# Splitting the store of the last group but one into unequal shares for the DMA engines

## The chip, the cores and the metric

The kernel runs on one core of one Trainium2 chip. The metric is the device time of one execution in microseconds: 209.35 us before the change, the median of 3 runs (209.31 to 209.42). The core has five engines that run their own instruction streams: PE (matrix multiplication), DVE, ACT and POOL (element-wise work) and SP, which here only issues transfers. Behind SP's queue stand 16 DMA engines that move the data between the chip's main memory (DRAM) and the on-chip memory of 128 partitions.

## The reference

```python
x        = randn(16, 512, 1024)   # float32
weight   = randn(1024, 768)
bias     = randn(768)
residual = randn(16, 512, 768)
out = (np.matmul(x, weight) + bias + residual).astype(np.float32)
```

Flattened, it is a product of 8192 x 1024 by 1024 x 768, to which a row (the bias) and a matrix of 8192 x 768 (the residual) are added.

## The kernel before

The 8192 rows are cut into 64 tiles of 128 rows (`n_sub`), eight of which make a group (`G = 8`, eight groups). Row p x 8 + j of a group lies in partition p, so that tile j of the group has one row in each partition, and the eight rows of a partition are contiguous in DRAM. One transfer of a group's residual or output therefore moves 128 pieces, one for each partition, of 8 x 768 x 4 = 24,576 bytes.

For each half group (four tiles) ACT casts x to bfloat16 (`cast_x`, L121), DVE transposes blocks of 32 x 32 (`transpose_blocks`, `transpose_and_move`, L152 to L161), ACT moves half of the blocks into place (`move_blocks`, L126), and PE multiplies with the weights (L307 to L326), tile by tile, into one of four PSUM buffers. DVE adds the PSUM buffers to the residual in place, two tiles at a time (`evacuate`, L163), and POOL adds the bias to the same place (`add_bias`, L212), two tiles at a time, 32 times in all. Tiles 62 and 63 get their bias before PE is done with them (addition 29, L224), so that the last step is DVE's. The place that held the residual then holds the output and is stored from there.

Every transfer is issued by SP, in the order of a list written by hand (`ORDER`, L17). A name such as `x5`, `r7` or `st6` stands for the load of x, the load of the residual or the store of that group; a letter stands for a part of its tiles, by `PARTS` and, for group 7, by `LAST_PARTS`: `st7a` is tiles 0 to 3, `st7b` 4 and 5, `st7c` 6 and 7. `st4+` stores groups 4 and 5 in one transfer. The loop at L240 takes the names in turn, lets SP wait for what the transfer needs, and issues it at L286. A store waits until POOL has counted its additions up to the last tile of the part (L278: the semaphore `add`, against the number kept in `added` for that tile), and the very last store waits for DVE (L276). All stores from group 3 on raise one semaphore, `st`, by 16 each (L284); the kernel ends when it has reached its full count (`late`, L35 and L39). Between the loads and the stores nothing else orders the transfers: SP's instructions run in order, and the DMA engines work through what they were given.

Of the kernel before, what the change touches and what calls it, by code (L numbers as in the profile page):

```python
# [11 lines left out]
P = 128  # L12
# [2 lines left out]
B = 4  # L15

ORDER = ("x0a w0 bias w1 x0b r0 x1a x1b r1 x2 r2 x3 r3 x4 st0 "  # L17
         "st1 r4 x5 r5 st2 x6a x6b r6 x7 r7 st3 st4+ st6 st7a st7b st7c").split()
PARTS = {"": (0, 8), "a": (0, 4), "b": (4, 8)}
LAST_PARTS = {"a": (0, 4), "b": (4, 6), "c": (6, 8)}  # L20


@with_exitstack
def kernel(
    ctx: ExitStack,
    tc: tile.TileContext,
    x: bass.AP,
    weight: bass.AP,
    bias: bass.AP,
    residual: bass.AP,  # L30
    out: bass.AP,
):
    nc = tc.nc
    stored = ctx.enter_context(nc.semaphore("st"))
    late = 16 * sum(name[:2] == "st" and int(name[2]) > 2 for name in ORDER)  # L35
    nc.scalar.sem_inc(stored, late)
    with tc.tile_critical(name="all", no_gpsimd_drain=True):  # L37
        emit(nc, ctx, x, weight, bias, residual, out, stored, late)
    nc.sync.wait_ge(stored, late)  # L39


def emit(nc, es, x, weight, bias, residual, out, stored, late):
# [8 lines left out]
    n_grp = n_sub // G  # L51
    n_bat = n_sub // B
    chunks = [(0, 512), (512, N - 512)]
    sp, act, dve, pool, pe = nc.sync, nc.scalar, nc.vector, nc.gpsimd, nc.tensor
# [18 lines left out]
    def sem(name):  # L73
        if name not in sems:
            sems[name] = es.enter_context(nc.semaphore(name))
        return sems[name]

    def wait(eng, name, value):
        eng.wait_ge(sem(name), value)  # L79
# [14 lines left out]
    def group(ap, g):  # L94
        return ap[g * G * P:(g + 1) * G * P, :].rearrange("(p j) k -> p j k", p=P)

    def span(start, size):
        return data[:, start:start + size] if isinstance(start, int) else data[:, bass.ds(start, size)]

    def x_home(g):  # L100
        return X0 - (g % 2) * X_SLOT

    def x_rows(start, j, n):
        return span(start + j * K, n * K).rearrange("p (t k) -> p t k", k=K)

    def r_home(g):

        return (g % 4) * R_SLOT + ((g + 1) // n_grp) * (X0 - 3 * R_SLOT)

    def r_rows(start, j, n):  # L110
        return span(start + j * N, n * N).rearrange("p (j n) -> p j n", n=N)
# [94 lines left out]
    for h in (0, 1):  # L206
        part = slice(h * (R // 2), (h + 1) * (R // 2))
# [10 lines left out]
    added = {}  # L218
# [13 lines left out]
    def load_into(name):  # L232

        before = landed.get(name, 0)
        landed[name] = before + 16
        if before:
            wait(sp, name, before)
        return name

    for name in ORDER:  # L240
        into = name
        if name == "bias":
            wait(sp, "ev", EV0)
            src, dst = bias[None, :].to_broadcast((P // Q, N)), bias_rows[0:P:Q, :]
        elif name[0] == "w":
            k0 = int(name[1]) * (R // 2)
            src, dst = w_rows[:, k0:k0 + R // 2, :], w_stage[:, k0:k0 + R // 2, :]
        elif name[0] == "x":
            g, part = int(name[1]), name[2:]
            j0, j1 = PARTS[part]  # L250
            if g > 1 and part != "b":
                wait(sp, "cast", 2 * (2 * g - 2))
            if g == 3:
                wait(sp, "wc", 2)
                whole = 16 * sum(n[0] == "x" and len(n) == 2 and int(n[1]) < n_grp - 1 for n in ORDER)
                sp.sem_inc(sem("xb"), whole)
                landed["xb"] += whole
            into = load_into("xb" if part == "b" else "xa")
            src, dst = group(x2d, g)[:, j0:j1, :], x_rows(x_home(g), j0, j1 - j0)
        elif name[0] == "r":  # L260
            g = int(name[1])
            if g == n_grp - 1:
                wait(sp, "cast", 2 * (2 * g))
                if f"x{g}" in ORDER:
                    sp.sem_inc(sem("xb"), 16)
            elif g > 3:
                wait(sp, f"st{g - 4}", 16)
            into = load_into("r")
            src, dst = group(res2d, g), r_rows(r_home(g), 0, G)
        else:  # L270
            g, part = int(name[2]), name[3:]
            n = 2 if part == "+" else 1
            j0, j1 = (LAST_PARTS if g == n_grp - 1 else PARTS)[part.strip("+")]
            end = (g + n - 1) * G + j1
            if end == n_sub:
                wait(sp, "ev", ev_end)  # L276
            else:
                wait(sp, "add", added[end - 1])  # L278
            src, dst = r_rows(r_home(g), j0, j1 - j0), group(out2d, g)[:, j0:j1, :]
            if n > 1:  # L280
                src = span(r_home(g), n * R_SLOT).rearrange("p (g k) -> p g k", g=n)
                dst = out2d[g * G * P:(g + n) * G * P, :].rearrange(
                    "(g p j) n -> p g (j n)", g=n, p=P)
            if g > 2:  # L284
                into = "st"
        sp.dma_start(out=dst, in_=src).then_inc(sem(into), 16)  # L286

    half_bytes = B * (R // 2) * P * 4
    xt_end = nc.lookup_mloc(xt).addr + (P - 1) * 4
# [17 lines left out]
    with pe.Fori(0, n_bat):  # L307
        tiles = iter(range(B))
        for i in range(B):
# [5 lines left out]
            for k in range(R):  # L315
                for c, (n0, nl) in enumerate(chunks):
                    ins = pe.add_instruction(mybir.InstMatmult(  # L317
                        name=nc.get_next_instruction_name(),
# [36 lines left out]
```

## Time and profile before

| what | value |
|---|---|
| median of 3 runs | 209.35 us (209.31 to 209.42) |
| profiled execution, own time | 209.55 us |
| its span, first to last instruction | 207.8 us |
| busy: PE, DVE, ACT, POOL | 82%, 80%, 70%, 56% of the span |
| DMA | 87.05 MB in 4456 packets, 419 GB/s over the span |
| issue of st3, st4+, st6 | 157.86, 162.62, 184.06 us |
| issue of st7a, st7b, st7c | 194.44, 198.47, 199.36 us |
| last matmul ends, last DVE addition ends | 198.34, 199.34 us |

A packet in the profile is one piece of a transfer on one DMA engine, here the row of one partition, or the four bytes with which an engine reports that its share is done. The DMA share is the mean busy share of the 16 engines: 1.00 is all of them, 0.06 is one. The profile does not number the engines. The 1.75 us between the profiled execution's time and its span lie outside what the instructions show. Times below are microseconds from the start of the span.

### The profile page before, as it was taken

The page shows a single profiled execution, that of the slowest core. Times are in us where ns is not written, and L with a number is a line of the kernel's source. Part 1 is how long each engine was busy: PE and PEld are TensorE (multiplying, and loading weights), DVE is VectorE, ACT ScalarE, POOL GpSimd, SP SyncE. Part 2 cuts the span into 40 slices and gives each one's busy share as a digit, 9 for nine tenths or more (in the row PEclk, how much of TensorE's full clock was granted, in tenths as well). Part 3 has the DMA queues.
Part 4 walks back from the last instruction along what each step waited for, and adds up shares of the span by engine and source line. Part 5 has one row for each costly group of instructions (what it writes and reads, how often), then busy time and mean ns, then how long its engine had stood idle before and what let it go on. Part 6 is the DMA issues. An engine that isn't in the chain of part 4 may idle for free.

```text
span 207.8 us, 2311 instructions
## 1 busy us (share of the span) xinstructions
PE 171.2 (82%) x1024; PEld 50.6 (24%) x512; DVE 166.4 (80%) x180; ACT 144.8 (70%) x162; POOL 115.5 (56%) x38
## 2 busy tenths in 40 slices
PE   0000999969998999999999999699999999999910
PEld 0000233313332333232322233122323233233300
DVE  1068498899889989999999969995999999994510
ACT  2357976988599696979697679788497969760000
POOL 0055007539391939193929484484809393899820
PEclk9999999999999999999999999889999999999995
DMA  6999999999999999999999999999999999999994
GB/s 214 426 431 443 431 429 426 445 448 448 404 404 479 393 440 423 456 393 445 450 402 461 404 450 440 404 420 453 435 427 418 435 454 416 416 454 426 414 418 186
DMA packets 4456, 87.05 MB, mean 419 GB/s; under 512 B 484, under 2 KB 484, under 8 KB 744
## 3 DMA queue, kind: packets, MB, share of 16 engines
q1 hardware_dynamic: 4456, 87.05, 98.1%
HBM read 61.88 MB, written 25.17 MB: 419 GB/s over the span
## 4 chain that ended last, share of the span: by engine, by line
DMA 57%; PE 16%; DVE 12%; issue 5%; ACT 4%; SPq 0%; DVEq 0%; ACTq 0%
DMA data<-in_x_dram 46%; PE po L317 16%; DMA out_dram<-data 11%; DVE xt L159 7%; DVE data L165 3%; ACT xb L123 2%; ACT xt L128 2%; DVE tq L153 2%; SPq L286 0%; DVEq L90 0%; DVEq L175 0%; ACTq L90 0%; SPq L79 0%; ACTq L139 0%; SPq L350 0%
## 5 line engine op out<-in xcount | busy, mean ns | idle before, releaser
L317 PE MATMUL po<-w_sb,xt 128*128 128x512 bf16 (+1 forms) x1024 | 171.2, 330 | 27.1 <-DVE xt L159 20.6
L214 POOL TENSOR_TENSOR data<-data,bias_bc 128x1536 f32<-128x1536 f32 x32 | 109.8, 3453 | 70.1 <-DVE data L165 70.0
L128 ACT COPY xt<-tq 32x512 uint32<-32x512 uint32 x128 | 78.9, 617 | 23.4 <-DVE tq L153 20.7
L159 DVE STREAM_TRANSPOSE xt<-xb 32x512 uint32<-32x512 uint32 x128 | 90.2, 704 | 4.6 <-ACT xb L123 2.7
L317 PEld LDWEIGHTS po<-w_sb,xt 128*128 x512 | 50.6, 99 | 147.2 <-issue 145.7
L123 ACT CAST xb<-data 128x2048 bf16 x32 | 64.8, 2074 | 15.9 <-DMA data<-in_x_dram 15.6
L165 DVE TENSOR_TENSOR data<-po,data 128x1536 f32 (+2 forms) x33 | 55.9, 1708 | 12.9 <-PE po L317 12.5
L153 DVE STREAM_TRANSPOSE tq<-xb 128x1024 uint32<-128x1024 uint32 x16 | 19.8, 1236 | 3.8 <-ACT xb L123 3.8
L209 POOL CAST w_sb<-data 128x3072 bf16<-128x3072 f32 x2 | 5.5, 2744 | 12.6 <-DMA data<-in_weight_dram 12.6
L170 DVE LOAD_MASK_SELECT bias_bc<-bias_rows x1 | 0.0, 14 | 10.3 <-DMA bias_rows<-in_bias_dram 10.3
L132 ACT ACT_TABLE_LOAD x1 | 1.3, 1283 | 1.0 <-SPq L37 1.0
L167 DVE MEMSET bias_rows<- 128x768 f32 x1 | 0.7, 698 | 1.2 <-SPq L37 1.2
L170 DVE STREAM_SHUFFLE bias_bc<-bias_rows 128x768 f32<-128x768 f32 x1 | 1.0, 1003 | 0.0
L339 POOL MEMSET const-float32-0.0<- 128x1 f32 x1 | 0.1, 98 | 0.2 <-issue 0.2
L132 ACT COPY warm<-const-float32-0.0 128x1 f32<-128x1 f32 x1 | 0.2, 191 | 0.0
L339 POOL MEMSET const-bfloat16-1.0<- 128x1 bf16 x1 | 0.1, 101 | 0.0
L339 POOL MEMSET const-uint8-127<- 128x1 uint8 x1 | 0.1, 101 | 0.0
L339 POOL MEMSET const-float32-1.0<- 128x1 f32 x1 | 0.1, 98 | 0.0
## 6 DMA issues: line engine op xcount, KB each, us to landing
data<-in_residual_dram SPq DMA_DIRECT2D x8, 3072.0 KB, 17.0
data<-in_x_dram SPq DMA_DIRECT2D x5, 4096.0 KB, 21.8
out_dram<-data SPq DMA_DIRECT2D x5, 3072.0 KB, 23.9
data<-in_x_dram SPq DMA_DIRECT2D x6, 2048.0 KB, 18.6
out_dram<-data SPq DMA_DIRECT2D x1, 6144.0 KB, 29.5
data<-in_weight_dram SPq DMA_DIRECT2D x2, 1536.0 KB, 11.8
out_dram<-data SPq DMA_DIRECT2D x1, 1536.0 KB, 8.8
out_dram<-data SPq DMA_DIRECT2D x2, 768.0 KB, 7.1
```

The costliest lines, as they stand in the source:

```text
L123: act.copy(out=xb[:, c], in_=part.rearrange("p t (a j r) -> p t j a r", j=R // 2, r=2)).then_inc(sem("cast"), 1)
L128: act.copy(out=xt[q * Q:(q + 1) * Q, half, :, :, m * Q:(m + 1) * Q], in_=tq[m * Q:(m + 1) * Q, :, :, q]).then_inc(sem("mv"), 1)
L132: act.copy(out=warm[:], in_=nc.const_aps.tensor(0.0, [P, 1], FP32))
L153: dve.transpose(out=tq[:], in_=xb_words(0)).then_inc(sem("tq"), 1)
L159: ins = dve.transpose(out=xt[q * Q:(q + 1) * Q, half, :, :, m * Q:(m + 1) * Q], in_=words[m * Q:(m + 1) * Q])
L165: dve.tensor_add(out=rt, in0=po[:, j % 4:j % 4 + n, :N], in1=rt).then_inc(sem("ev"), 1)
L167: dve.memset(bias_rows[:], 0.0).then_inc(sem("ev"), EV0)
L170: dve.stream_shuffle(out=bias_bc[:], in_=bias_rows[:], mask=[0] * 32).then_inc(sem("bb"), 1)
L209: pool.tensor_copy(out=w_sb[:, part, :], in_=w_stage[:, part, :]).then_inc(sem("wc"), 1)
L214: pool.tensor_add(out=rt, in0=rt, in1=bias_bc[:, None, :].to_broadcast((P, 2, N))).then_inc(sem("add"), 1)
L317: ins = pe.add_instruction(mybir.InstMatmult(name=nc.get_next_instruction_name(), ins=[pe.lower_ap(w_sb[:, k, n0:n0 + nl]), stationary(i, k)],
L339: nc = _bacc.Bacc("TRN2", target_bir_lowering=False, num_devices=1)
```

## The change

The store of group 6, one transfer of 128 partitions by eight tiles, becomes six transfers. `st6a` stores tiles 0 to 4 of all 128 partitions (15,360 bytes from each). `st6b` stores tiles 5 to 7 (9216 bytes from each partition) in five transfers, issued one behind the other: partitions 0 to 111 in the first, then partitions 112, 116, 120, 124; 113, 117, 121, 125; 114, 118, 122, 126; and 115, 119, 123, 127. The bytes stored are the same.

Three things go with it. A part that ends on an odd number of tiles waits for the addition that covers the pair its last tile is in (`(end - 1) | 1`): `st6a` ends with tile 4 of the group and waits for the addition of tiles 4 and 5. The transfers of `st6b` have one wait, ahead of the first. And `late` counts transfers instead of names, since each of the five raises `st` by 16.

```diff
 ORDER = ("x0a w0 bias w1 x0b r0 x1a x1b r1 x2 r2 x3 r3 x4 st0 "
-         "st1 r4 x5 r5 st2 x6a x6b r6 x7 r7 st3 st4+ st6 st7a st7b st7c").split()
+         "st1 r4 x5 r5 st2 x6a x6b r6 x7 r7 st3 st4+ st6a st6b st7a st7b st7c").split()
 PARTS = {"": (0, 8), "a": (0, 4), "b": (4, 8)}
 LAST_PARTS = {"a": (0, 4), "b": (4, 6), "c": (6, 8)}
+SIX_PARTS = {"a": (0, 5), "b": (5, 8)}
+SPLIT = "st6b"
+WIDE, STEP = 112, 4
+
+
+def shares(name):
+    if name != SPLIT:
+        return [slice(0, P)]
+    return [slice(0, WIDE)] + [slice(WIDE + m, P, STEP) for m in range(STEP)]
...
-    late = 16 * sum(name[:2] == "st" and int(name[2]) > 2 for name in ORDER)
+    late = 16 * sum(len(shares(name)) for name in ORDER if name[:2] == "st" and int(name[2]) > 2)
...
-            j0, j1 = (LAST_PARTS if g == n_grp - 1 else PARTS)[part.strip("+")]
+            j0, j1 = {n_grp - 2: SIX_PARTS, n_grp - 1: LAST_PARTS}.get(g, PARTS)[part.strip("+")]
             end = (g + n - 1) * G + j1
             if end == n_sub:
                 wait(sp, "ev", ev_end)
             else:
-                wait(sp, "add", added[end - 1])
+                wait(sp, "add", added[(end - 1) | 1])
...
-        sp.dma_start(out=dst, in_=src).then_inc(sem(into), 16)
+        for rows in shares(name):
+            sp.dma_start(out=dst[rows] if name == SPLIT else dst,
+                         in_=src[rows] if name == SPLIT else src).then_inc(sem(into), 16)
```

## The prediction

> **What bounds the kernel now.** I read the page from its end, because the change touches only the last stores. First the busy share of the DMA engines (part 3) and the slices of part 2.
>
> ```profile
> PEclk9999999999999999999999999889999999999995
> DMA  6999999999999999999999999999999999999994
> ...
> DMA packets 4456, 87.05 MB, mean 419 GB/s; under 512 B 484, under 2 KB 484, under 8 KB 744
> ## 3 DMA queue, kind: packets, MB, share of 16 engines
> q1 hardware_dynamic: 4456, 87.05, 98.1%
> ```
>
> The 16 DMA engines are busy 98.1% of the span and no slice but the first and the last falls below 9 tenths. So the kernel is bound by the engines' own time, and only three things can shorten it: fewer bytes, the head, or the tail. The bytes stay. Each engine moves 87.05 MB / 16 = 5.44 MB in 0.981 x 207.8 = 203.9 us, 26.7 GB/s.
>
> Next the tail, by windows cut where the traffic falls (columns from the left: window, length, busy time of PE, PEld, DVE, ACT, POOL with counts, clock, DMA share, GB/s).
>
> ```profile
> 190.00:199.00 9.00, 8.34 (x52) 2.39 (x25) 3.34 (x3) 0.00 (x0) 7.84 (x3) 1.00 1.00 427
> 199.00:204.40 5.40, 0.00 (x0) 0.00 (x0) 0.34 (x1) 0.00 (x0) 0.00 (x0) 0.75 1.00 422
> ...
> 204.60:204.80 0.20, 0.00 (x0) 0.00 (x0) 0.00 (x0) 0.00 (x0) 0.00 (x0) 0.50 0.75 307
> 204.80:205.00 0.20, 0.00 (x0) 0.00 (x0) 0.00 (x0) 0.00 (x0) 0.00 (x0) 0.50 0.16 62
> 205.00:205.20 0.20, 0.00 (x0) 0.00 (x0) 0.00 (x0) 0.00 (x0) 0.00 (x0) 0.50 0.08 31
> 205.20:205.40 0.20, 0.00 (x0) 0.00 (x0) 0.00 (x0) 0.00 (x0) 0.00 (x0) 0.50 0.07 31
> ...
> 206.20:206.40 0.20, 0.00 (x0) 0.00 (x0) 0.00 (x0) 0.00 (x0) 0.00 (x0) 0.50 0.07 31
> 206.40:206.60 0.20, 0.00 (x0) 0.00 (x0) 0.00 (x0) 0.00 (x0) 0.00 (x0) 0.50 0.00 0
> ```
>
> All 16 work until 204.6. Then they stop within half a microsecond, and from 205.1 to 206.47 the share is 0.07, which is 1/16 and one row of 6144 B at a time: **one engine works alone for about 1.36 us.** Last packet 206.47, span 207.8: 1.3 us of confirmation and closing follow, and stay.
>
> The packet records of the trace, followed from each packet to the one that starts where it ends, show how this engine came to be late. Up to 85 us, with loads alone, all 16 stay within 0.45 us of each other. In the stores it loses some 0.2 us for every 3 MB: its rows of 24,576 B take 0.935 us on average between 170 and 199 us, those of the others 0.912. In the last four stores its completion counts 1.38, 1.39, 1.40 and 1.47 us after the next-latest engine's.
>
> The chain of waits ends in PE and the last DVE additions, and the last store is indeed issued late, at 199.36. That does not set the end:
>
> ```profile
> out_dram<-data SPq DMA_DIRECT2D x1, 1536.0 KB, 8.8
> out_dram<-data SPq DMA_DIRECT2D x2, 768.0 KB, 7.1
> bias_rows<-in_bias_dram SPq DMA_DIRECT2D x1, 12.0 KB
> ```
>
> 768 KB at 427 GB/s is 1.8 us, yet they take 7.1 to land: some 5 us of it is standing in line behind earlier rows. The first load takes 1.0 us from issue (0.96) to first packet; the last store's first row starts no earlier than 202.83 on any engine (records), 2.4 us after 199.36 + 1.0.
>
> **The change, part by part.** *How a transfer falls on engines.* Part 6 counts 30 transfers of 128 partitions and the bias of four; 484 packets under 512 B are completions: 30 x 16 + 4. So a transfer of 128 rows uses 16 engines with eight rows each, and one of four rows uses four engines. I take 112 rows as seven on each of 16, and the four small ones as one row on each of the same four engines, four rows in all. By the records the late engine carried none of the four bias rows. [...]
>
> *Row times.* From the records, start to start: 6144 B 0.231, 12,288 B 0.457, 24,576 B 0.908 us, so about 5 ns fixed and the rest in proportion. 15,360 B then is 0.569 and 9216 B 0.344 (9216 / 26.7 GB/s from the page gives 0.345). A completion packet adds 6 ns.
>
> *Engines that lose a row* (twelve, the late one with them): before 8 x 0.908 = 7.266. After 8 x 0.569 + 7 x 0.344 + 0.006 = 6.966. Gain 0.30; with 2.5% slow rows 0.31. The late engine ends at 206.47 - 0.31 = 206.16.
>
> *The four that get four extra rows:* 8 x 0.569 + 11 x 0.344 + 5 x 0.006 = 8.364, a loss of 1.10. All engines but the late one are done by 205.11, so they end by 206.21 at most and by 205.75 at least (204.65 + 1.10).
>
> *Bounds of that.* No row here shows long transfers whose partitions fall on the engines other than eight apiece. The lower end of the cost is no slowing, as above. The nearest row is the bias load: its rows go to partitions 0, 32, 64 and 96 beside full-size weight rows on the other engines, and each took 0.121 us, which is 3072 B at the usual pace; no packet beside them was longer by more than 0.036. The upper end is every one of the eleven rows at half pace, for two engines that fetch through one path: 11 x 0.344 = 3.8 us. I take no slowing, the row that there is.
>
> *SP.* Five more issues, each 0.33 to 0.34 us by the issue rows. The first half of the store needs the addition of tiles 4 and 5 only:
>
> ```profile
> 177.18 17.23 POOL L214 TENSOR_TENSOR data<-data,bias_bc 128x1536 f32<-128x1536 f32 x5 [4.20 <-DVE data L165]
> ```
>
> Counting back from the 32nd and last addition (195.01), these five are 27 to 31. Addition 27 ends at 180.62, 28 at 184.06, when the whole store is issued now. So st6a goes at 180.65, and its 112 rows and four small ones at 184.06 to 185.8. The next instruction on SP, st7a, waits for addition 31 at 194.41 and is issued at 194.44: 8.6 us of room hide the five. Behind the wait stand st6b, st7a to c and the closing wait, and none moves. If that cover were gone it would cost up to 5 x 0.34 = 1.7 us of issue; engines are at that time 6 us behind the issue, so even then nothing. Engines that come 0.3 us earlier to st7a (first row now 197.32, 2.9 us after its issue) and st7b (200.98, 2.5 after) still find it ready, since a row can start 1.0 after its issue. PE, ACT, DVE and POOL have the same instructions.
>
> *Sum.* The end moves from 206.47 to the later of 206.16 and at most 206.21: -0.26 to -0.31; I take -0.30, since only one of 15 engines ends as late as 205.11. Profiled span 207.5, profiled time 209.25 against 209.55. The median of the runs shown is 209.35, 0.20 under the profiled run: **209.05**, -0.14%. About 0.2% (0.42 us) is what a measurement of this kernel can tell from no change, so this counts as no change.
>
> **The rivals.** *Rows that collide, slower.* [...] If two readers of neighbouring partitions share one path of one engine's pace, the four extra rows at half pace cost 4 x 0.344 = 1.38 more: 205.11 + 1.10 + 1.38 = 207.59, +1.1, 210.45 us. If all eleven rows suffer: 205.11 + 1.10 + 3.78 = 209.99, +3.5, 212.9. It decides as soon as the four engines lose more than 0.26 us over their eleven rows (7% of their time). [...]
>
> *The late engine is an effect of the profiler, or one of the four; slower.* Then nobody is late whom the change relieves, and the four lose 1.10 of which up to 0.46 is slack: +0.6 to +1.1, 210.0 to 210.45. Against: without that 1.36 us a plain run should be near 208.2; the median is 209.35.
>
> *It does not do what it says: the 112 rows do not go seven by seven.* If the last 16 partitions are wholly those of four engines, the late one among them, these lose four rows (-1.36) and the four gain four (205.11 + 1.42 = 206.53, or 206.1 if none of them is the latest): -0.4 to +0.1, about 209.2.
>
> **How the numbers follow.** Chances: the forecast 0.40, collisions 0.40, no late engine to relieve 0.10, other shares of rows 0.10. The likeliest one's own range is 208.9 to 209.2 (its sum, and the 0.1 by which the runs differ). The whole range reaches from 208.9 over the second and third case into the first rival, to 212.0; what lies above (most rows colliding) and below is about 0.15. Faster by over 0.2%: 0.08, from the forecast's and last rival's edges. Within: 0.33 of the forecast, 0.07 of the last rival, a little of mild collisions, 0.42. Slower: 0.37 of collisions, 0.10 of the second rival and the rest, 0.50.
>
> **What would show it.** In the profile after: 4616 packets, 516 under 512 B (484 + 32). The tail by windows: two to five engines stop together near 206.1 instead of one alone at 206.47; then the forecast is right. If four engines work alone (share 0.25) past 206.5 and rows of 9216 B take well over 0.35 us, rows collide; with rows at 0.35 and the four alone from 205, the late engine was none. SP's issue of st7a at 194.4 shows the issues hidden; later by a microsecond and a gap in the DMA share before 198, and that step was wrong. The forecast falls with any fall of the share below 0.9 between 188 and 204.

## The result and the profile after

The changed kernel takes **210.16 us** (median of 7 runs, 210.05 to 210.41), the kernel before beside it 209.42 (7 runs): ratio 1.0034, 95% interval 1.0024 to 1.0044. It is 0.7 us slower, where 0.3 faster was forecast. The profiled execution has 210.05 us and a span of 208.3.

The transfers fell on the engines as the working had it. First the packet line of the page, then SP's issues (start, duration) of st6a, of st6b, and of st7a (each line marked x2 is one stretch of two issues, and the next line starts with its second):

```profile
DMA packets 4616, 87.05 MB, mean 418 GB/s; under 512 B 516, under 2 KB 516, under 8 KB 776
```

```profile
178.86 0.34 SPq L296 DMA_DIRECT2D out_dram<-data  x1
...
182.26 1.09 SPq L296 DMA_DIRECT2D out_dram<-data  x2
182.65 1.56 SPq L296 DMA_DIRECT2D out_dram<-data  x2
183.39 1.68 SPq L296 DMA_DIRECT2D out_dram<-data  x2
184.25 1.69 SPq L296 DMA_DIRECT2D out_dram<-data  x2
...
192.63 0.34 SPq L296 DMA_DIRECT2D out_dram<-data  x1
```

4616 packets and 516 completions are the forecast numbers: sixteen engines for the 112 rows, four for each small transfer. POOL's additions came 1.8 us earlier in this execution, and SP with them: in the profiled execution before, the granted clock fell to 0.91 between 120 and 140 us, in this one it stayed at 1.00. The end came later all the same, so it is not the computation that sets it. The five issues of st6b lie between 182.26 and 185.94, st7a follows at 192.63. They are hidden, though the four small ones took about 0.8 us each ((185.94 - 182.65) / 4), not the 0.33 to 0.34 of the working.

The tail (columns as before; the DMA share is the last but one):

```profile
204.60:205.20 0.60, 0.00 (x0) 0.00 (x0) 0.00 (x0) 0.00 (x0) 0.00 (x0) 0.50 0.40 164
205.20:205.80 0.60, 0.00 (x0) 0.00 (x0) 0.00 (x0) 0.00 (x0) 0.00 (x0) 0.50 0.34 143
205.80:206.40 0.60, 0.00 (x0) 0.00 (x0) 0.00 (x0) 0.00 (x0) 0.00 (x0) 0.50 0.15 61
206.40:207.00 0.60, 0.00 (x0) 0.00 (x0) 0.00 (x0) 0.00 (x0) 0.00 (x0) 0.50 0.07 31
207.00:207.60 0.60, 0.00 (x0) 0.00 (x0) 0.00 (x0) 0.00 (x0) 0.00 (x0) 0.50 0.00 0
```

From 205.2 to 205.8 five engines work (0.34 x 16 = 5.4), as forecast: the late one and the four with extra rows. But they do not stop together. From 206.4 one of them is alone again (0.07), until 207.1, where the late engine of before stopped at 206.47. The end moved by +0.63 us (the profiled time by +0.50, from 209.55 to 210.05).

Which one it is, and why, is in the packet records of the trace. The rows of 9216 B on these five engines, in their order, times in us (a row that meets nothing takes 0.347 from its start to its end; the next starts 0.344 after it), and the end of each engine's last packet:

```
engine                  seven rows of the wide transfer   four extra rows               end
with extra rows, A      7 x 0.347                         0.347 0.672 0.711 0.914       207.11
with extra rows, B      7 x 0.347                         0.347 0.347 0.347 0.627       206.06
with extra rows, C      7 x 0.347                         0.347 0.347 0.347 0.411       206.17
with extra rows, D      7 x 0.347                         0.347 0.347 0.347 0.347       205.91
the late engine         0.348 0.347 0.449 0.685, 3 x 0.347                              206.43
```

Engine A lost 0.672 + 0.711 + 0.914 - 3 x 0.347 = 1.26 us on three rows; without that it would have ended at 205.85. The late engine lost 0.44 on two, without which it would have ended at 205.99. So even with A undisturbed the kernel would have gained no more than 0.04 (206.47 to 206.43). Of the 112 rows of the wide transfer 107 took 0.347 to 0.348.

The ten long rows, five of the sixteen extra ones and five of the wide transfer, lie between 195.5 and 199.8 us, and most overlap: from 197.4 to 198.0 three are under way at once, on A, on the late engine and on a third, and from 198.3 to 198.7 three again, on A, B and C. Eleven of the sixteen engines were in st7a by 198.0 (its first row starts at 197.08).

### The profile page after: what moved, and what is told of

Its sections match the earlier page's. It is cut to its first block, busy times and chain, and to the rows that moved or that the text cites. A ratio compares the mean times of both kernels' runs of the same rounds, so it can differ in the third digit from the quotient of the medians.

```text
span 208.3 us, 2316 instructions
## 1 busy us (share of the span) xinstructions
PE 170.6 (82%) x1024; PEld 50.6 (24%) x512; DVE 166.3 (80%) x180; ACT 144.9 (70%) x162; POOL 115.5 (55%) x38
## 2 busy tenths in 40 slices
DMA packets 4616, 87.05 MB, mean 418 GB/s; under 512 B 516, under 2 KB 516, under 8 KB 776
## 3 DMA queue, kind: packets, MB, share of 16 engines
q1 hardware_dynamic: 4616, 87.05, 97.9%
## 4 chain that ended last, share of the span: by engine, by line
DMA 77%; PE 10%; DVE 4%; issue 2%; ACT 1%; SPq 0%; DVEq 0%; ACTq 0%
DMA data<-in_x_dram 65%; DMA out_dram<-data 11%; PE po L328 10%; DVE xt L168 2%; DVE data L174 1%; ACT xb L132 1%; DVE tq L162 1%; SPq L296 0%; DVEq L99 0%; SPq L88 0%; ACTq L99 0%; SPq L361 0%; SPq L46 0%
```

## The experiments

All were built from the changed kernel by the function `shares`, which says how st6b is dealt out, and by the tiles of `SIX_PARTS`. Each ratio is to the kernel before, run beside it. K, P and W are the three theories that the first expectation names. After the first, a diff shows the line that comes in for the last one of `shares` (one for each run where two stand together) and, where it changes, `SIX_PARTS`. Times of single rows are from the records of the one profiled execution of each kernel.

**1. Only split by tiles.**

```diff
-    return [slice(0, WIDE)] + [slice(WIDE + m, P, STEP) for m in range(STEP)]
+    return [slice(0, P)]
```

> The store of group 6 is split by tiles only (five and three), all of it on 128 partitions; nothing goes to four engines. Three theories for the 0.7 us that the change lost against a forecast gain of 0.3. K (collisions): rows that different engines read at one time from the same partitions' neighbourhood hamper each other. P (pieces): more transfers cost, wherever they lie. W (wide): the 112 rows of seven each are slow by themselves. K and W expect here only the eight more row starts at 5 ns and a completion packet: +0.04, 209.46 us, and one engine alone at the end for about 1.4 us as before. P expects part of the loss, 209.6 us.

Measured 209.44 us, ratio 0.9999 (0.9990 to 1.0007). The split itself costs nothing that can be seen, as K and W have it, and the tail is that of before:

```profile
205.40:205.80 0.40, 0.00 (x0) 0.00 (x0) 0.00 (x0) 0.00 (x0) 0.00 (x0) 0.50 0.07 31
205.80:206.20 0.40, 0.00 (x0) 0.00 (x0) 0.00 (x0) 0.00 (x0) 0.00 (x0) 0.50 0.07 31
206.20:206.60 0.40, 0.00 (x0) 0.00 (x0) 0.00 (x0) 0.00 (x0) 0.00 (x0) 0.50 0.00 0
```

One engine is alone, until 206.35. The whole loss lies in the dealing out.

**2. The last 16 partitions in one transfer.**

```diff
+    return [slice(0, WIDE), slice(WIDE, P)]
```

> As the changed kernel, but the last 16 partitions go in one transfer of 16 in place of four of four. If 16 rows use 16 engines, each has 7 + 1 rows again, so the shares are even, the late engine is not relieved and ends about 1.4 us after the rest. K and P expect 209.5 us (+0.05 of row starts and completions; K some tenths more if single rows collide). W expects the long rows of the 112 again: four of them were found in the changed kernel, costing the engines that had them 0.14, 0.44 and 0.76 us, the 0.44 on the late engine, so 209.9 us.

Measured 210.17 us, ratio 1.0039 (1.0013 to 1.0064), with a wide spread (209.25 to 212.13). In the records of its profiled execution (210.21) the late engine sets the end, at 207.27, and the time went where W put it: its wide rows took 0.35, 0.37, 0.53, 0.91, 0.35, 0.35 and 0.39 us, its row of the last 16 0.47, together 0.9 us more than undisturbed. But on the other 15 engines 104 of 105 wide rows took 0.347 (one 0.54). The 112 rows are not slow by themselves, then; in this execution they were so for the engine that goes through them last, 1.4 us behind the others. (Being last is not enough: in run 3 the late engine's wide rows took at most 0.39.) Long are also five rows of the 16-row transfer on engines that have room for it: 1.53, 1.38, 1.32, 0.90 and 0.55. The five overlap in time (197.1 to 198.7). Of sixteen rows that lie side by side, one to an engine, three took about four times as long (4 x 0.347 = 1.39). K had foreseen neither in this size; W came nearest to the number (209.9), but its reason holds for one engine only.

**3. The small transfers on partitions 0 to 15.** Sizes, number and order as in the changed kernel.

```diff
+    return [slice(P - WIDE, P)] + [slice(m, P - WIDE, STEP) for m in range(STEP)]
```

> The four small transfers take partitions 0 to 15 (m, m+4, m+8, m+12) and the wide one 16 to 127; sizes, number and order are those of the changed kernel. K, with the four engines being those that read partitions 0 to 15 in the other stores too: none of the sixteen rows meets another engine's, they take 0.347 us each, the four engines end near 206.1 and the late one near 206.2: 209.1 us, 0.3 under the kernel before. K, with four other engines: no difference to the changed kernel. P and W: 210.1 us as the changed kernel.

Measured **209.17 us**, ratio 0.9989 (0.9980 to 0.9997). All sixteen extra rows take 0.347. The tail:

```profile
204.60:205.20 0.60, 0.00 (x0) 0.00 (x0) 0.00 (x0) 0.00 (x0) 0.00 (x0) 0.50 0.40 164
205.20:205.80 0.60, 0.00 (x0) 0.00 (x0) 0.00 (x0) 0.00 (x0) 0.00 (x0) 0.50 0.32 133
205.80:206.40 0.60, 0.00 (x0) 0.00 (x0) 0.00 (x0) 0.00 (x0) 0.00 (x0) 0.50 0.05 21
206.40:207.00 0.60, 0.00 (x0) 0.00 (x0) 0.00 (x0) 0.00 (x0) 0.00 (x0) 0.50 0.00 0
```

Five engines (0.32) work until 206, and none after 206.1: their last packets end at 206.01, 206.03, 206.04, 206.05 and 206.09. This is the picture that was forecast for the changed kernel, where the number of bytes, rows and transfers is the same. P falls with it, and so does W, for which the 112 rows would be slow here too (one of the 105 on the other engines was long, 0.43). So does the rival that the lateness is made by the profiler: plain runs then would have lost about 1 us to the four engines, and they gained 0.2.

**4. 120 partitions and eight, one tile.**

```diff
-SIX_PARTS = {"a": (0, 5), "b": (5, 8)}
+SIX_PARTS = {"a": (0, 7), "b": (7, 8)}
...
+    return [slice(0, 120), slice(120, P)]
```

> Tests whether the late engine is late in plain runs too. Tiles 0 to 6 of group 6 go as one transfer, tile 7 (rows of 3072 B, 0.121 us each) as 120 partitions and 8. If a transfer uses the largest number of engines up to 16 that divides its rows, 120 rows go to 15 engines with eight rows each, and 8 rows to 8 engines. If the engine left out is the late one and it is late in plain runs too: it ends 8 x 0.121 = 0.97 us earlier, the others at most 0.2 later, so the end moves from 206.47 to about 205.5: 208.5 us. If lateness is an effect of the profiler, or another engine is left out: 209.5 us. If rows collide on the 15 engines at half pace (K at its worst): the others end 0.97 + 0.2 later, about 206.3, so 209.2 us. [...]

Measured 209.67 us, ratio 1.0010 (1.0001 to 1.0018). One engine indeed had none of the 120 rows: it ended at 204.06, 0.65 us or more ahead of the rest (eight rows of 0.121 are 0.97). It is not the late one, which had nine rows in place of eight and ended at 206.57. The forecast of 209.5 for that case is 0.17 low; that row is 0.12 of it.

**5. Small transfers of four partitions side by side.**

```diff
+    return [slice(0, WIDE)] + [slice(WIDE + STEP * m, WIDE + STEP * (m + 1)) for m in range(STEP)]
```

> The changed kernel with the partitions dealt out differently: the small transfers take 112 to 115, 116 to 119, 120 to 123 and 124 to 127, so that each one's four rows lie side by side. K, in the form that partitions side by side share one path of one engine's pace: four rows at a time queue on one path, the last of them takes 4 x 0.347 = 1.39 us, and an engine that comes last four times loses 4 x 1.04 = 4.2 us on top of the 1.1 of the extra rows: end at 205.1 + 1.1 + 4.2 = 210.4, 213.3 us; 211 us if the places in the queue change from transfer to transfer. If rows only meet those of other stores: 210.2 us, as the changed kernel.

Measured 211.83 us, ratio 1.0111 (1.0097 to 1.0126): slower than four apart by 1.7 us, with nothing changed but which of the sixteen partitions go together. Extra rows of 1.57, 1.41, 1.31, 1.28 and 1.24 us stand in the records, again about four times 0.347. The number lies between the two of K, but not because the places change from transfer to transfer: one of the four engines has 0.347 four times, and the other three lose 1.5, 2.2 and 2.9 us on their extra rows, most of it on the first two and less on the later ones (1.57, 1.31, 0.79 and 0.62 on the worst). The late engine loses 0.8 in its wide rows as well and ends at 207.17. The tail has four engines, these three and the late one, where before it had one:

```profile
205.80:206.40 0.60, 0.00 (x0) 0.00 (x0) 0.00 (x0) 0.00 (x0) 0.00 (x0) 0.50 0.27 113
206.40:207.00 0.60, 0.00 (x0) 0.00 (x0) 0.00 (x0) 0.00 (x0) 0.00 (x0) 0.50 0.27 113
207.00:207.60 0.60, 0.00 (x0) 0.00 (x0) 0.00 (x0) 0.00 (x0) 0.00 (x0) 0.50 0.17 72
207.60:208.20 0.60, 0.00 (x0) 0.00 (x0) 0.00 (x0) 0.00 (x0) 0.00 (x0) 0.50 0.12 51
208.20:208.80 0.60, 0.00 (x0) 0.00 (x0) 0.00 (x0) 0.00 (x0) 0.00 (x0) 0.50 0.05 20
```

**6 and 7. The small transfers on 32 to 47, and on 64 to 79.**

```diff
+    return [slice(0, 32), slice(48, P)] + [slice(32 + m, 48, STEP) for m in range(STEP)]
...
+    return [slice(0, 64), slice(80, P)] + [slice(64 + m, 80, STEP) for m in range(STEP)]
```

> The small transfers take partitions 32 to 47 (32+m, 36+m, 40+m, 44+m); the rest goes as 0 to 31 and 48 to 127, two and five rows on each engine. K, if the four engines read 32 to 47 in the other stores as they do 0 to 15: no long rows among the sixteen, 209.2 us plus 0.02 for one more completion. If it is the lowest partitions alone that are free, or if the place at the end of the order matters: 210.1 us. [...]

> As the run with 32 to 47, but the small transfers take 64 to 79, and the rest goes as 0 to 63 and 80 to 127, four and three rows on each engine. K: partitions that four other engines read in the neighbouring stores, so long rows again as with 112 to 127: 209.8 to 210.5 us. If two wide transfers or another place than 112 free the rows: 209.2 us.

On 32 to 47: 209.47 us, ratio 1.0002 (0.9993 to 1.0010). All sixteen extra rows take 0.347, as K has it, and yet 0.3 us were lost. In the profiled execution, at 209.89 slower than the median, all 14 long rows (0.48 to 1.2 us) lie in the wide transfer of 80 rows, a dealing that had not been used before, and an engine without extra rows ends last. On 64 to 79: 211.76 us, ratio 1.0107 (1.0093 to 1.0122), above K's range. 38 of the 128 rows were long, those of the wide transfers as well as the extra ones, and rows of the stores behind them, so this run tells less of the extra rows than was meant: two causes lie in it. In the tail nearly all engines are late, not four:

```profile
204.60:205.20 0.60, 0.00 (x0) 0.00 (x0) 0.00 (x0) 0.00 (x0) 0.00 (x0) 0.50 0.93 389
205.20:205.80 0.60, 0.00 (x0) 0.00 (x0) 0.00 (x0) 0.00 (x0) 0.00 (x0) 0.50 0.86 358
205.80:206.40 0.60, 0.00 (x0) 0.00 (x0) 0.00 (x0) 0.00 (x0) 0.00 (x0) 0.50 0.59 246
```

**8. Six tiles shared out on 0 to 15.**

```diff
-SIX_PARTS = {"a": (0, 5), "b": (5, 8)}
+SIX_PARTS = {"a": (0, 2), "b": (2, 8)}
...
+    return [slice(P - WIDE, P)] + [slice(m, P - WIDE, STEP) for m in range(STEP)]
```

> The small transfers on partitions 0 to 15 as before, but six tiles instead of three are shared out (st6a two tiles, rows of 18,432 B, 0.683 us). Tests the sizes of the sum where nothing collides. The late engine goes 0.63 us down from 206.47, to 205.84; the four engines, which ended at 206.01 to 206.08 with three tiles, take three more rows of 0.34 each: 207.1, and set the end alone, with the others done by 205.1: 1.0 us over the run with three tiles, 210.2 us.

Measured 210.91 us, ratio 1.0072 (1.0057 to 1.0086), 0.7 more than expected. The four engines ended at 206.85, 207.03, 207.30 and 207.90 where the sum had 207.1 for all. The first three bear the sum out within 0.25, and the late engine, at 205.68, is 0.16 ahead of it. The fourth came out of the wide transfer 0.9 us late: near the end of that (196 to 197 us) six rows of 18,432 B took 0.76 to 1.6 us in place of 0.686.

**9 and 10. The small transfers first,** on 112 to 127 and on 0 to 15.

```diff
+    return [slice(WIDE + m, P, STEP) for m in range(STEP)] + [slice(0, WIDE)]
...
+    return [slice(m, P - WIDE, STEP) for m in range(STEP)] + [slice(P - WIDE, P)]
```

> The changed kernel with the order within the store turned round: the four small transfers (112 to 127) first, the wide one last. K: the rows of the small transfers now meet the rows of st6a on the engines that read 112 to 127 there, and the four engines come to the wide one 1.4 us after the others, no longer in step with them: long rows as before or more, 209.8 to 211 us. If it is st7a behind them that they collide with, and only that: no long rows, 209.2 us.

> The small transfers on partitions 0 to 15, ahead of the wide one (16 to 127). The sixteen rows should stay at 0.347 us as in the run with the other order. What is tested is the wide transfer: so far its rows were short as long as the engines went through it together, and long where some had moved on or came later. If being in step is what spares them, the four engines, now 1.4 us behind in it, meet the others: several long rows of 0.5 us and more, 209.4 to 210.5 us. If the order is indifferent: 209.2 us.

On 112 to 127: 210.89 us, ratio 1.0067 (1.0041 to 1.0092), in K's range, but not as K had it. Of the 17 long rows one is a small one (0.581); the other fifteen small rows took 0.347, and the 16 long rows left (0.40 to 1.54) lie in the wide transfer. Ahead of the wide transfer the small rows on 112 to 127 met next to nothing. That points to st7a, which ran beside them in the changed kernel, as what they met there. On 0 to 15: 209.86, ratio 1.0016 (1.0005 to 1.0028), in the range expected, but its profiled execution (209.48) shows all sixteen small rows at 0.347 and a single long row of 9216 B (0.946). Several long rows, as the idea of engines in step would have it, were not seen. Why this order loses 0.5 to 0.7 us on the other one (209.33 in run 12, 209.17 in run 3) is not settled.

**11. Two tiles, transfers of seven rows.**

```diff
-SIX_PARTS = {"a": (0, 5), "b": (5, 8)}
+SIX_PARTS = {"a": (0, 6), "b": (6, 8)}
...
+    return [slice(32, P)] + [slice(m, 28, STEP) for m in range(STEP)] + [slice(28, 32)]
```

> Two tiles are shared out: 32 to 127 in one transfer (six rows on each engine), then four transfers of seven rows (m, m+4, ..., m+24) and one of four (28 to 31). Tests which of the first eight engines the late one is, and whether more engines can carry its rows. If it is the eighth, transfers of seven rows pass it by: 8 x 0.683 + 6 x 0.231 + 0.006 = 6.86 in place of 7.27, it ends at 206.06; the first four end at 205.11 + 0.78 = 205.9; 209.0 us, or 209.5 if the last four rows, which lie side by side, queue on one path (0.7 more on the last of them). If it is the fifth to seventh, it gets ten rows in place of eight: 206.47 + 0.5 = 207.0, 209.9 us. [...]

Measured 210.02 us, ratio 1.0023 (1.0015 to 1.0032): the second case, 209.9. The late engine had four extra rows and is alone for longer than ever:

```profile
205.80:206.40 0.60, 0.00 (x0) 0.00 (x0) 0.00 (x0) 0.00 (x0) 0.00 (x0) 0.50 0.08 31
206.40:207.00 0.60, 0.00 (x0) 0.00 (x0) 0.00 (x0) 0.00 (x0) 0.00 (x0) 0.50 0.07 31
207.00:207.60 0.60, 0.00 (x0) 0.00 (x0) 0.00 (x0) 0.00 (x0) 0.00 (x0) 0.50 0.05 20
```

One engine (0.07) from 206.0 to 207.68. This profiled execution, 210.65, is the slowest of the twelve. So the late engine is one of the seven that a seven-row transfer uses and not one of the four that a four-row transfer uses, if the sets start at the same engine. Its 207.68 is 0.7 above the 207.0 of that case, 0.37 of it on one long row (0.609 for 0.234). The two kernels that give the late engine more work (this and the fourth) made plain runs slower, the third, which took work from it, made them faster: it sets the end in plain runs.

**12. The third once more.**

> The kernel with the small transfers on 0 to 15 behind the wide one, once more, beside the others of this call: 209.17 us again, 0.1% under the kernel before.

Measured 209.33 us (209.06 to 210.19), ratio 0.9993 (0.9982 to 1.0004). Its profiled execution, 209.43, had two long rows in the wide transfer (0.58 and 0.94). The two runs of this kernel together say: clearly faster than the changed kernel (by 0.8 to 1.0 us), and 0.07 to 0.11% under the kernel before, which only the first of them tells from none.

## Why the prediction was wrong

**What bounds the kernel** was right: the tail of the DMA engines, one of them late by 1.4 us, in plain runs as under the profiler. Runs 3, 4 and 11 moved that engine's share, and the time went the way its share went (in run 4 by little: 1.0001 to 1.0018).

**How a transfer falls on engines** was right: 516 completions. The 112 rows went seven to each of 16 engines, and the four small transfers to the same four, A to D, with four extra rows each. The transfer of 120 rows in run 4 left one engine out, as a division among 15 has it. A rule for sizes that were not run is not shown.

**The row times and the sum of rows** were right. Engine D, which met nothing, ended at 205.91, within the 205.75 to 206.21 of the working, and A would have at 205.85. In run 3 the end moved to 206.09, -0.38 where -0.26 to -0.31 was worked out; in plain runs it and run 12 gave 0.23 and 0.12, less than the 0.30 forecast.

**SP's issues hidden** was right: all out by 185.94, st7a at 192.63. Their size was not: the five took 3.7 us, where the working had up to 5 x 0.34 = 1.7. The row to go by was the issue of the bias load, also of four rows, at 0.65 us; the 6.7 us of room left hid the difference.

**The step that failed** is the choice between the bounds: "I take no slowing, the row that there is." The upper end, eleven rows at half pace, was too much; none was not enough. Five of the sixteen extra rows and five of the 112 were long, engine A's three by 1.26 us, and the kernel's end is the end of its slowest engine: one engine of four that loses on three rows is all it takes. The row that it was rested on, the bias load, has rows of 3072 B (0.121 us), a third as long, and is a load where the extra rows are stores. Run 4, a store with rows of that size, had four long ones, of which the worst lost 0.22 us, so being short did not keep them clear. It was the nearest row, and it was too far. The chances were better than the choice: the same working gave collisions 0.40, as much as the forecast, and a slower kernel 0.50.

What came about was the first rival, rows that collide, and its point of decision (0.26 us on the four engines) was well passed. Its price, +1.1 us, was for four extra rows at half pace on an engine that ends last of the 15; three rows at about half pace or less, on one that ends in the middle, gave +0.63 to the end and +0.74 to the time. Half pace was the author's estimate, and no run shows it as a fixed price: the long extra rows took 0.411 to 0.914 us in the changed kernel and up to 1.57 in run 5, for 0.347. The rival had priced only the four engines and left out the late one, which lost 0.44 in the wide rows. Run 5, with the wide transfer untouched, and run 3 show that it is the choice of partitions: equal sizes, numbers and order, and 209.2, 210.2 or 211.8 us by which partitions go together and to which engine. That the rows wait for a path to the on-chip partitions is not shown: each partition's row also has its own place in DRAM, every run moved the two together, and a clash on the DRAM side stays possible. What the runs show is that of rows that lie side by side and are read at one time some took 1.24 to 1.57 us, about 4 x 0.347 (runs 2 and 5), and that the sixteen extra rows on 32 to 47 took 0.347 (run 6), as on 0 to 15.

The second rival (the late engine made by the profiler, or one of the four) gave nearly the time measured, 210.0 to 210.45, for a reason that run 3 and the table of rows exclude: the late engine had no extra row. The third would have shown four engines near 206.5 and the late one relieved by four rows; the late engine had seven, as the table of rows shows.

Open stay: on which side the rows clash, which engine reads which partitions (K's readers in the other stores are a supposition), why of the four engines with extra rows A has three long ones and D none, why the late engine is slow in stores and not in loads, and what run 10 loses.

## What to carry to other kernels

Where 16 engines end a kernel together, look at the tail window by window: a share of 1/16 at the end (here 0.07 for 1.36 us) is one engine to be relieved, and its length is all that can be won. Work can be moved between engines by the number of rows of a transfer, but the partitions have to be chosen by trial: on 0 to 15 and 32 to 47 all sixteen extra rows of 9216 B ran undisturbed (0.347 us), on 112 to 127 (up to 0.914) and 64 to 79 they did not, and the slowest of the engines took the gain and more. The gain at best was 0.1%. A short row that runs undisturbed beside others (3072 B in 0.121 us) does not say that a long one will (9216 B in up to 0.914 us).

## What was not expected of the hardware

- Rows of neighbouring partitions at one time did not take equally long. In run 2 eleven of the sixteen rows took at most 0.47 us and three 1.32 to 1.53; in run 5 one engine had 0.347 four times while the other three lost 1.5 to 2.9 us. That one is served while the others wait would fit these times, but is not shown.
- One engine is slow in stores (0.935 us for rows of 24,576 B against 0.912; with loads alone, up to 85 us, it kept within 0.45 us of the others). It had none of the rows of the four-row transfers in the changed kernel, a share of the 120 rows and of the eight in run 4 (nine rows in place of eight), and four extra rows from the seven-row transfers of run 11. That makes it one of the fifth to seventh only if transfers of few rows all start at the first engine, which no view shows.
- In runs 3, 4, 8, 10 and 12 twelve rows of the wide transfer were long on engines other than the late one (0.43 us for 0.347 in run 3, up to 1.6 for 0.686 in run 8), and each was the last of its engine in that transfer. In run 6, where the wide part went as two and five rows an engine, 14 were long (0.48 to 1.2 us), and not only last ones. No run shows why.
